# The small products of a delta-net at other places in the program

## The chip, the core and the metric

The kernel runs on one core of a Trainium2 chip. Its time is the device time of one execution in microseconds (us). TensorE (PE) does the matmuls and transposes, VectorE (DVE) the elementwise work and the rounding remainders, ScalarE (ACT) functions and copies, GpSimd (POOL) a few elementwise steps; SyncE (SP) issues the DMAs.

## What is computed

Four decoder layers on x of 256 tokens by 1024 channels, float32. Each adds half a SwiGLU FFN (1024 to 2816 and back), a mixer, and half of a second FFN; a last RMS norm ends it. Layer i has mixer i mod 3: the gated delta-net in layers 0 and 3, stick-breaking attention in 1, sparse attention in 2. The change touches the delta-net alone:

```python
def gated_deltanet(h, w_in, conv_w, a_log, dt_bias, norm_g, w_out):
    proj = h @ w_in                                  # q, k, v, gate z, and 8+8 columns for beta and decay
    qkv = silu(causal_depthwise_conv(proj[..., :3 * GDN_DIM], conv_w))     # 4 taps
    q, k, v = 8 heads of 128 each;  q = l2norm(q) * 128 ** -0.5;  k = l2norm(k)
    beta = sigmoid(b_logit);  g = -exp(a_log) * softplus(a + dt_bias)
    o = chunk_gated_delta_rule(q, k, v, g, beta)     # triangular solves, then a recurrence
    o = rmsnorm(o, norm_g) * silu(z)
    return o @ w_out
```

h is the normalised x. The kernel multiplies the gain in first and the row factor 1/rms after the projections.

## The kernel before

**Matmuls in three parts.** Float32 products are made of three matmuls of a reduced type: a weight is split into a hi half (`h`, ACT, line 175) and a lo half (`l`, DVE, line 176), x likewise, and `mm3` adds hi*hi, lo*hi and hi*lo. All matmuls are issued in line 43 and all transposes in line 56, so a row is told by its tiles, not by its line. A weight chunk of 1 MB (128 x 2048) is loaded by one DMA, split in four pieces of 512 columns, and gives a tile of 256 output channels by 256 tokens: 2 halves x 8 k tiles x 3 = 48 matmuls of 256 columns into a bank of tag G. There are three raw buffers, ten for hi and ten for lo halves, and four PSUM banks each of tags G and A.

**The delta-net.** `gdn_order` lists 16 projection chunks as (kind, c), kind 0 for keys, 1 values, 2 queries, 3 gates; a chunk c holds two heads. After each chunk comes its follow-up: `conv2` (a multiply with the norm factor, four taps on ACT, POOL and DVE, Silu) for keys, values and queries, a multiply and Silu for gates. Then generators do the small products with banks of tag A. `rstd` sums the squares of x and makes the norm factor `rb` by a rsqrt of nine small DVE steps and a transpose ("spread", line 242). `gates` makes beta, the decays and the matrices E, and needs `rb`. `keys(c)` transposes the keys (`bk`, line 488), sums their squares on ACT (492), takes a rsqrt on DVE (line 494; steps of lines 213 to 217), waits for the gates, and after a lag `g_new` scales `bk` (501), spreads the rsqrt (502), scales the keys (503), and multiplies them with themselves (509); from there a triangular inverse goes by doubling. `queries(c)` transposes and multiplies with the keys; `delta(c)` waits for all inverses and is a chain of small products, the last of which waits for the gate of c. `out_proj` multiplies the heads with the output weights, with banks of tag G.

**Order.** The program is written out by a planner. `mm` adds 256/2400 to `now` for a matmul of 256 columns. A generator yields a lag after which its next step is due (or a condition); `add` gives the first lag. `pump`, called after every second k tile of a projection, runs the steps that are due, from the first six generators. `wait` runs steps until a condition holds, with `now` set ahead. A compiler pass then orders each engine's instructions by this order of the program and by its own estimate of when operands are there; each engine works through its own queue in that order.

```python
    g_key, g_val, g_qry, g_del, g_new, g_inv, g_out, g_mul = 9.0, 6.0, 6.0, 8.0, 2.8, 1.0, 7.5, 1.0
            yield self.g_new
            self.wait(lambda: "rb" in st)
                self.add(keys(c), self.g_key)
```

These are the lag of the keys' second step (276, 500), the wait for the norm behind the first chunk (655), and the first lag of the keys (666).

Of the kernel before, what the change touches and what calls it, by code (L numbers as in the profile page):

```python
# [20 lines left out]
P = 128  # L21
T = 256
D = 1024
KT = D // P
# [41 lines left out]
class Trunk:  # L66
# [177 lines left out]
    def rstd(self, st, lat=4.6, power=False):  # L244
# [18 lines left out]
        else:  # L263
# [9 lines left out]
    lag, width, burst = 1.0, 6, 5  # L273
    lat_sum, lat_power = 5.2, 2.4
    dsa_width = 4
    g_key, g_val, g_qry, g_del, g_new, g_inv, g_out, g_mul = 9.0, 6.0, 6.0, 8.0, 2.8, 1.0, 7.5, 1.0
    s_qk, s_sp, s_att = 2.5, 5.5, 1.3

    gdn_order = ((0, 0), (0, 1), (0, 2), (3, 0), (0, 3), (3, 1), (2, 0), (1, 0), (1, 1), (1, 2), (1, 3),
                 (2, 1), (3, 2), (2, 2), (2, 3), (3, 3))  # L280
    korder = (0, 2, 4, 6, 1, 3, 5, 7)

    def tiles2(self, pieces, xg, order=None):

        b = self.bank("G")
        for m in range(2):
            for q, j in enumerate(order or self.korder):
                b.mm3(b.t[:, m * T:(m + 1) * T], self.sub(pieces, m * D + j * P, P), xg[j], q == KT - 1)
                if q % 2:
                    self.pump()  # L290
        return b
# [89 lines left out]
    def gdn(self, i, n):  # L381
        nc, a = self.nc, self.a
# [10 lines left out]
        bah, bal = self.small("bah", [P, 8, 16], F32R, 1), self.small("bal", [P, 8, 16], F32R, 1)  # L393
        self.split(bah, bal, wba)
        xg = self.norm_in(n)
        st = {}
        self.add(self.rstd(st))


        bba = self.bank()  # L400
        for j in range(KT):
            bba.mm3(bba.t[:16, :T], (bah[:, j], bal[:, j]), xg[j], j == KT - 1)


        four = lambda name: self.big.tile([P, 4, 4, P], F32, name=name, tag="b8")
        LL = self.big.tile([P, 4, 2, 4, P], F16, name="LL", tag="b8")
        XX = self.big.tile([P, 4, 2, 4, P], F16, name="XX", tag="b8")
# [8 lines left out]
        dl, ea = self.small("dl", [P, 4, 2], bufs=1), self.small("ea", [P, 4, 2], bufs=1)  # L416

        def gates():
            ba = self.pad
            nc.vector.tensor_mul(ba[:16], bba.t[:16, :T], st["rb"][:16])  # L420
            bt = self.bank()
            for t in range(2):
                bt.tr(bt.t[:, t * P:(t + 1) * P], ba[:, t * P:(t + 1) * P])
            v = bt.v4()[:, :2, :16].rearrange("p t (s c m) -> p s c t m", s=2, c=4)
            self.act_set("natural_log_exp_and_others")
            for t in range(2):
                nc.scalar.activation(beta[:, :, t], v[:, 0, :, t], AF.Exp, scale=-1.0)
                nc.vector.tensor_add(z[:, :, t], v[:, 1, :, t], ad[:, 1].rearrange("p (c m) -> p c m", m=2))
            nc.vector.tensor_scalar(beta, beta, 1.0, None, op0=ALU.add)
            nc.vector.reciprocal(beta, beta)  # L430
            nc.scalar.activation(e, z, AF.Abs)
            nc.scalar.activation(e, e, AF.Exp, scale=-1.0)
            nc.scalar.activation(e, e, AF.Ln, bias=self.ones[:, :1])
            nc.vector.scalar_tensor_tensor(sp, z, 0.0, e, op0=ALU.max, op1=ALU.add)
            self.tc.keep_in_program_order(nc.scalar.activation(ea, ad[:, 0].rearrange("p (c m) -> p c m", m=2), AF.Exp))
            for t in range(2):
                nc.vector.scalar_tensor_tensor(g[:, :, t], sp[:, :, t], -1.0, ea, op0=ALU.mult, op1=ALU.mult)
            yield 3.0
            bg = self.bank()
            bg.mm(bg.t[:, :16], triu, g.rearrange("p c t m -> p (c t m)"))  # L440
            bg.mm(bg.t[:, 16:24].rearrange("p (c m) -> p c m", m=2), self.ones, g[:, :, 0])
            G = bg.t[:, :16].rearrange("p (c t m) -> p c t m", c=4, t=2)
            nc.vector.tensor_scalar(nG, G, -1.0, None, op0=ALU.mult)
            nc.vector.tensor_add(dl, bg.t[:, 16:24].rearrange("p (c m) -> p c m", m=2), nG[:, :, 0])
            nc.scalar.activation(dl, dl, AF.Exp)
            nc.scalar.activation(eG, G, AF.Exp)
            nc.vector.tensor_copy(e, G)

            for c in range(4):
                yield 0.8  # L450
                b = self.spread([e[:, c, t, m:m + 1] for t in range(2) for m in range(2)])
                nc.scalar.activation(eGb[:, c], b.v4()[:, 2:], AF.Exp)
                nc.vector.tensor_add(E[:, c], b.v4(), nG[:, c].rearrange("p t m -> p (t m)")[:, :, None].to_broadcast([P, 4, P]))
                nc.gpsimd.affine_select(out=E[:, c], in_=E[:, c], compare_op=ALU.is_ge, fill=-BIG, base=0, pattern=[[0, 4], [1, P]],
                                        channel_multiplier=-1)
                nc.scalar.activation(E[:, c], E[:, c], AF.Exp)
            self.act_set("silu_and_others")
            st["gates"] = True
# [3 lines left out]
        def conv2(b, kind, c, dst):  # L462

            pc = self.pcs[cnt[0] % 2]
            cnt[0] += 1
            nc.vector.tensor_mul(pc[:, :, 3:], b.v2(), st["rb"][:, None, :].to_broadcast([P, 2, T]))  # L466

            base = (1, 2, 0)[kind] * 8 + 2 * c
            w = lambda m, o: conv[:, base + m, o:o + 1]
            tap = self.w5("tap").rearrange("p (m t) -> p m t", m=2)  # L470
            for m in range(2):
                nc.scalar.activation(dst[:, m], pc[:, m, 0:T], AF.Copy, scale=w(m, 0))
                nc.scalar.activation(tap[:, m], pc[:, m, 1:1 + T], AF.Copy, scale=w(m, 1))
            nc.gpsimd.tensor_add(dst, dst, tap)
            for m in range(2):
                for o in (2, 3):
                    nc.vector.scalar_tensor_tensor(dst[:, m], pc[:, m, o:o + T], w(m, o), dst[:, m], op0=ALU.mult, op1=ALU.add)  # L477
            nc.scalar.activation(dst, dst, AF.Silu)
# [7 lines left out]
        def keys(c):  # L486
# [10 lines left out]
            nc.gpsimd.tensor_mul(A, E[:, c], beta[:, c].rearrange("p t m -> p (t m)")[:, :, None].to_broadcast([P, 4, P]))  # L497
            ks = self.small("ks", [P, 2], tag="ms")
            nc.vector.tensor_mul(ks, y[:, :2], dl[:, c])
            yield self.g_new  # L500
            nc.vector.tensor_mul(kx[:, 0, c], bk.v4()[:, :2], ks[:, :, None].to_broadcast([P, 2, P]))
            b = self.spread([y[:, t * 2 + m:t * 2 + m + 1] for m in range(2) for t in range(2)])
            nc.vector.tensor_mul(k2, k2, b.v2())
# [16 lines left out]
            b = self.bank()  # L520
# [27 lines left out]
            b = self.bank()  # L548
# [6 lines left out]
            for src, dst in ((XT, X1), (X1, XF[:, c])):  # L555
                yield self.g_inv
                b = self.bank()
# [6 lines left out]
        def values(c, vT):  # L564
            b = transposed(vT)
            nc.scalar.activation(v[:, c], b.v4(), AF.Copy)
            st["v", c] = True
            yield 0
# [82 lines left out]

        heads, gz = {}, {}
        for kind, c in self.gdn_order:
            b = self.tiles2(self.chunk(a["gdn_in"][i, kind * 4 + c], pool=self.pool_lo), xg)
            self.wait(lambda: "rb" in st)
            if kind == 0:
                if c == 0:
                    self.add(gates())
                    late = b
                    continue  # L660
                if c == 1:
                    self.wait(lambda: "gates" in st)
                    conv2(late, 0, 0, kT[:, 0:2])
                    self.add(keys(0), self.g_key)
                conv2(b, 0, c, kT[:, 2 * c:2 * c + 2])
                self.add(keys(c), self.g_key)
            elif kind == 1:
                vT = self.w5("vT").rearrange("p (m t) -> p m t", m=2)
                conv2(b, 1, c, vT)
                self.add(values(c, vT), self.g_val)  # L670
            elif kind == 2:
                conv2(b, 2, c, qT[:, 2 * c:2 * c + 2])
                if c == 0:
                    oh, ol = self.b8("oh", F32R), self.b8("ol", F32R)
                self.add(queries(c), self.g_qry)
                self.add(delta(c), self.g_del)
            else:
                gz[c] = self.small("z", [P, 2, T], bufs=4)
                nc.vector.tensor_mul(gz[c], b.v2(), st["rb"][:, None, :].to_broadcast([P, 2, T]))
                nc.scalar.activation(gz[c], gz[c], AF.Silu)  # L680
# [537 lines left out]
```

## Time and profile before

| | |
|---|---|
| runs | 2054.35, 2075.12, 2082.24 us; median 2075.12 |
| profiled execution | 2066.59 us, of which 2064.6 us are the span of its instructions |
| PE, DVE, ACT, POOL busy in the span | 97%, 78%, 63%, 8% |
| granted TensorE clock | 0.996 of full speed, mean of the span |

Times in rows are microseconds from the start of the span, durations in ns where marked. A wait is idle time of an engine right before an instruction, put down to what released it. PE's ends are modelled and matmuls overlap, so their spacing is read from starts.

### The profile page before, as it was taken

What the parts mean: (1) busy time and instruction counts of PE and PEld (TensorE: products, weight loads), DVE (VectorE), ACT (ScalarE), POOL (GpSimd) and SP (SyncE); (2) the same over time, 40 slices, a digit from 0 to 9 for tenths busy, and PEclk for the clock granted to TensorE, in tenths of its full rate; (3) what the DMA queues carried; (4) which work ended last, traced back from release to release, by engine and by line L of the source; (5) the groups of instructions that cost most, each with busy time, mean ns of one, the idle gap of its engine ahead of it and who ended that gap; (6) DMA issues with size and microseconds to landing.
All of it is one profiled execution on the core that took longest, in us unless ns stands there. A gap on an engine that the chain in (4) does not pass through costs nothing.

```text
span 2064.6 us, 43653 instructions
## 1 busy us (share of the span) xinstructions
PE 2009.8 (97%) x17578; PEld 1978.6 (96%) x17578; DVE 1603.2 (78%) x3413; ACT 1305.8 (63%) x2804; POOL 163.8 (8%) x150
## 2 busy tenths in 40 slices
PE   8999899999999999999999998999999998999998
PEld 8999889999999989999999997999999998999998
DVE  8778898877877776866787779877787789988665
ACT  6656776666666666655666665666666667766554
POOL 1001411100100010100010023100010014201000
PEclk9999999999999999999999999999999999999999
DMA  7554323555555543555555542455555543235552
GB/s 273 191 199 170 107 104 124 184 195 193 180 209 186 202 168 139 196 184 184 184 190 199 187 161 88 165 187 201 189 195 190 198 170 103 103 123 184 184 184 82
DMA packets 52619, 353.93 MB, mean 171 GB/s; under 512 B 6976, under 2 KB 7872, under 8 KB 10688
## 3 DMA queue, kind: packets, MB, share of 16 engines
q1 hardware_dynamic: 52128, 350.49, 47.9%
q8 instruction: 137, 2.24, 0.4%
q10 hardware_dynamic: 288, 0.66, 0.1%
q14 instruction: 66, 0.54, 0.1%
HBM read 350.07 MB, written 1.05 MB: 170 GB/s over the span
## 4 chain that ended last, share of the span: by engine, by line
PE 83%; DVE 11%; ACT 3%; issue 2%; POOL 1%; DMA 0%; SPq 0%; ACTq 0%; DVEq 0%; POOLq 0%
PE bankG L43 56%; PE bankA L43 26%; DVE l L176 4%; ACT x L227 1%; DVE kT L477 1%; PE bankA L56 1%; ACT h L175 1%; DVE x L228 1%; DVE qT L477 0%; DVE x L313 0%; DVE rs_y L217 0%; DVE vT L477 0%; DVE pc L466 0%; DVE rs_t L215 0%; ACT sq L249 0%
## 5 line engine op out<-in xcount | busy, mean ns | idle before, releaser
L43 PE MATMUL bankG<-x,h 128*128 128x256 f32 x7008 | 1257.3, 280 | 9.1 <-ACT x L227 6.1
L176 DVE TENSOR_TENSOR l<-r,h 128x512 fp32r<-128x512 f32 x1328 | 936.2, 713 | 398.9 <-ACT h L175 396.8
L175 ACT ACTIVATE h<-r 128x512 fp32r<-128x512 f32 x1328 | 822.1, 626 | 575.7 <-PE bankG L43 329.1
L43 PEld LDWEIGHTS bankG<-x,h 128*128 128x128 f32 x7008 | 1077.6, 189 | 11.5 <-ACT x L227 6.4
L43 PE MATMUL bankG<-x,l 128*128 128x256 f32 x3504 | 978.4, 279 | 0.1
L43 PEld LDWEIGHTS bankG<-x,l 128*128 128x128 f32 x3504 | 659.9, 188 | 0.4 <-DVE l L176 0.3
L43 PE MATMUL bankA<-ah,h 128*128 128x256 f32 x1408 | 390.9, 278 | 0.0
L43 PE MATMUL bankA<-al,h 128*128 128x256 f32 x1408 | 390.9, 278 | 0.0
L43 PE MATMUL bankA<-ah,l 128*128 128x256 f32 x1408 | 390.8, 278 | 0.0
L43 PEld LDWEIGHTS bankA<-al,h 128*128 128x128 f32 x1408 | 266.0, 189 | 0.1
L43 PEld LDWEIGHTS bankA<-ah,h 128*128 128x128 f32 x1408 | 264.4, 188 | 0.1
L43 PEld LDWEIGHTS bankA<-ah,l 128*128 128x128 f32 x1408 | 264.4, 188 | 0.0
L341 DVE TENSOR_TENSOR e<-e,bankG 128x256 f32<-128x256 f32 x352 | 145.5, 414 | 0.9 <-ACT e L340 0.9
L340 ACT ACTIVATE e<-bankG 128x256 f32<-128x256 f32 x352 | 133.3, 379 | 7.9 <-PE bankG L43 6.3
L250 POOL TENSOR_TENSOR sq<-sq 128x512 f32<-128x512 f32 x12 | 15.5, 1290 | 1445.0 <-ACT sq L249 1445.0
L353 DVE TENSOR_TENSOR e<-e,rb 128x512 f32<-128x512 f32 x176 | 119.8, 685 | 0.0
L204 ACT ACTIVATE ah<-e 128x256 fp32r<-128x256 f32 x176 | 73.2, 417 | 22.1 <-DVE e L355 22.0
L354 ACT ACTIVATE e<-e 128x256 f32<-128x256 f32 x176 | 70.9, 404 | 14.3 <-DVE e L353 14.3
L355 DVE TENSOR_TENSOR e<-e 128x256 f32<-128x256 f32 x176 | 73.6, 419 | 0.5 <-ACT e L354 0.5
L205 DVE TENSOR_TENSOR al<-e,ah 128x256 fp32r<-128x256 f32 x176 | 73.6, 419 | 0.5 <-ACT ah L204 0.5
L43 PE MATMUL bankG<-oh,h 128*128 128x256 f32 x256 | 73.1, 286 | 0.1
L43 PE MATMUL bankG<-oh,l 128*128 128x256 f32 x256 | 71.3, 279 | 0.0
(292 smaller groups left out, 1683.0 us busy)
## 6 DMA issues: line engine op xcount, KB each, us to landing
r<-in_ffn SPq DMA_DIRECT2D x262, 1024.0 KB, 4.8
r<-in_gdn_in SPq DMA_DIRECT2D x32, 1024.0 KB, 4.8
r<-in_gdn_out SPq DMA_DIRECT2D x8, 1024.0 KB, 4.8
r<-in_sb_qk SPq DMA_DIRECT2D x8, 1024.0 KB, 4.8
r<-in_sb_v SPq DMA_DIRECT2D x4, 1024.0 KB, 5.0
r<-in_sb_out SPq DMA_DIRECT2D x4, 1024.0 KB, 4.8
r<-in_dsa_out SPq DMA_DIRECT2D x4, 1024.0 KB, 5.3
r<-in_dsa_in SPq DMA_DIRECT2D x3, 1024.0 KB, 4.8
```

The lines of the kernel that those rows point to most:

```text
L43: self.nc.tensor.matmul(out, lhsT, rhs, start=self.fresh, stop=stop, skip_group_check=True)
L56: self.nc.tensor.transpose(out, x, self.k.ident)
L175: self.nc.scalar.activation(h[:, :pw], src, AF.Copy)
L176: (self.nc.gpsimd if pool else self.nc.vector).tensor_sub(l[:, :pw], src, h[:, :pw].bitcast(F32))
L204: self.nc.scalar.activation(dh, src, AF.Copy)
L205: self.nc.vector.tensor_sub(dl, src, dh.bitcast(F32))
L227: self.nc.scalar.activation(xh, self.x[:, j], AF.Copy, scale=g)
L340: nc.scalar.activation(e[:, m * T:(m + 1) * T], b.t[:, :T], AF.Copy)
L341: nc.vector.tensor_add(e[:, m * T:(m + 1) * T], e[:, m * T:(m + 1) * T], b.t[:, T:])
L353: nc.vector.tensor_mul(e2, e2, st["rb"][:, None, :].to_broadcast([P, 2, T]))
L354: nc.scalar.activation(e[:, :T], e[:, :T], AF.Silu)
L355: nc.vector.tensor_mul(e[:, T:], e[:, T:], e[:, :T])
```

## The change

Six edits, all in the delta-net. The 24 small matmuls for beta and decay come behind the first projection chunk instead of ahead of it. That first chunk runs its k tiles in the outer loop, both halves of the output for each. The wait for the norm factor comes behind the second chunk instead of the first; `gates` is added behind the first and holds itself until `rb` is there. `g_new` is 4.8 instead of 2.8, and 3.0 more for chunk 0. The first lag of the keys of chunk 1 is 4.0 longer. In `gdn_order` the query chunks (2,2) and (2,3) come ahead of gate chunk (3,2).

```diff
-    g_key, g_val, g_qry, g_del, g_new, g_inv, g_out, g_mul = 9.0, 6.0, 6.0, 8.0, 2.8, 1.0, 7.5, 1.0
+    g_key, g_val, g_qry, g_del, g_new, g_inv, g_out, g_mul = 9.0, 6.0, 6.0, 8.0, 4.8, 1.0, 7.5, 1.0
...
-                 (2, 1), (3, 2), (2, 2), (2, 3), (3, 3))
+                 (2, 1), (2, 2), (2, 3), (3, 2), (3, 3))
...
-    def tiles2(self, pieces, xg, order=None):
+    def tiles2(self, pieces, xg, order=None, first=False):
...
+        if first:
+            for q, j in enumerate(self.korder):
+                w = [self.sub(pieces, m * D + j * P, P) for m in range(2)]
+                for i, o in ((0, 0), (1, 0), (0, 1)):
+                    for m in range(2):
+                        b.mm(b.t[:, m * T:(m + 1) * T], w[m][i], xg[j][o], q == KT - 1 and o == 1)
+                self.pump()
+            return b
...
-        bba = self.bank()
-        for j in range(KT):
-            bba.mm3(bba.t[:16, :T], (bah[:, j], bal[:, j]), xg[j], j == KT - 1)
...
         def gates():
+            yield lambda: "rb" in st
             ba = self.pad
...
-            yield self.g_new
+            yield self.g_new + (3.0 if c == 0 else 0.0)
...
-            b = self.tiles2(self.chunk(a["gdn_in"][i, kind * 4 + c], pool=self.pool_lo), xg)
+            b = self.tiles2(self.chunk(a["gdn_in"][i, kind * 4 + c], pool=self.pool_lo), xg, first=(kind, c) == (0, 0))
+            if kind == 0 and c == 0:
+
+                bba = self.bank()
+                for j in range(KT):
+                    bba.mm3(bba.t[:16, :T], (bah[:, j], bal[:, j]), xg[j], j == KT - 1)
+                self.add(gates())
+                late = b
+                continue
             self.wait(lambda: "rb" in st)
             if kind == 0:
-                if c == 0:
-                    self.add(gates())
-                    late = b
-                    continue
...
-                self.add(keys(c), self.g_key)
+                self.add(keys(c), self.g_key + (4.0 if c == 1 else 0.0))
```

## Rows read from the trace of the kernel before

**Rows 1.** The page: engines busy in the span, and the chain that ended last.

```profile
PE 2009.8 (97%) x17578; PEld 1978.6 (96%) x17578; DVE 1603.2 (78%) x3413; ACT 1305.8 (63%) x2804; POOL 163.8 (8%) x150
...
PE 83%; DVE 11%; ACT 3%; issue 2%; POOL 1%; DMA 0%; SPq 0%; ACTq 0%; DVEq 0%; POOLq 0%
```

**Rows 2.** Waits of PE, 184 to 362 (total, times, longest); then layer 3, 1672 to 1854.

```profile
PE bankA L56 <- DVE rs_y L217: 3.5, 4, 1.8
PE bankA L56 <- ACT kT L478: 3.1, 1, 3.1
PE bankA L56 <- DVE rs_t L216: 2.7, 1, 2.7
PE bankA L56 <- ACT qT L478: 2.2, 1, 2.2
...
PE bankA L56 <- DVE rs_y L217: 3.6, 4, 1.9
```

**Rows 3.** Delta-net in stretches: PE, PEld, DVE, ACT, POOL busy (count); clock, DMA.

```profile
184.00:200.00 16.00, 15.83 (x137) 14.96 (x137) 15.06 (x27) 12.56 (x23) 5.33 (x4) 1.00 0.32 111
200.00:224.00 24.00, 20.12 (x170) 19.36 (x169) 19.09 (x45) 16.19 (x39) 8.96 (x9) 1.00 0.40 147
224.00:236.00 12.00, 9.29 (x81) 9.13 (x80) 11.22 (x36) 10.70 (x34) 3.07 (x3) 0.97 0.26 89
236.00:248.00 12.00, 10.92 (x85) 10.48 (x84) 11.47 (x32) 6.96 (x18) 4.42 (x5) 0.88 0.25 89
248.00:270.00 22.00, 20.20 (x232) 19.27 (x231) 20.80 (x53) 15.16 (x37) 7.32 (x5) 1.00 0.35 124
270.00:300.00 30.00, 29.49 (x403) 27.77 (x404) 27.46 (x74) 20.57 (x53) 4.33 (x4) 1.00 0.16 55
```

**Rows 4.** Line 176 alone in a stretch: DVE busy (count), clock, DMA.

```profile
180.00:190.40 10.40, 3.91 (x6) 1.00 0.59 202
```

**Rows 5.** Tile l in stretches: PE, PEld, DVE busy (count), clock, DMA.

```profile
190.40:219.70 29.30, 17.67 (x63) 11.66 (x62) 11.80 (x14) 1.00 0.40 144
219.70:229.90 10.20, 4.72 (x18) 3.33 (x18) 1.94 (x2) 1.00 0.01 2
229.90:241.00 11.10, 2.94 (x11) 1.98 (x11) 4.89 (x8) 0.85 0.54 190
241.00:270.00 29.00, 15.82 (x55) 10.29 (x55) 8.00 (x12) 1.00 0.27 94
270.00:294.40 24.40, 7.33 (x23) 4.44 (x24) 1.36 (x2) 1.00 0.05 21
294.40:326.00 31.60, 15.22 (x55) 10.34 (x55) 14.80 (x21) 1.00 0.49 174
```

**Rows 6.** Chain in order of time: one chunk back to back in layer 0 (start, us).

```profile
49.13 5.44 PE bankA L43 x48
```

**Rows 7.** Timeline of PE: two spreads (start, us; idle before and its releaser).

```profile
203.01 0.43 PE L56 MATMUL bankA<-ident,rs_y 128*128 128x128 f32 x2 [0.60 <-DVE rs_y L217]
...
235.59 1.09 PE L56 MATMUL bankA<-ident,rs_y 128*128 128x128 f32 x4 [2.71 <-DVE rs_t L216]
```

**Rows 8.** Timeline of ACT: Silu of key chunk 1.

```profile
222.79 0.63 ACT L478 ACTIVATE kT<-kT 128x512 f32<-128x512 f32 x1 [2.29 <-DVE kT L477]
```

**Rows 9.** Timeline of DVE, 224 to 238.

```profile
224.78 1.38 DVE L176 TENSOR_TENSOR l<-r,h 128x512 fp32r<-128x512 f32 x1 [2.08 <-ACT h L175]
226.08 2.44 DVE L477 SCALAR_TENSOR_TENSOR kT<-pc,conv,kT 128x256 f32<-128x256 f32 x4
...
229.34 0.68 DVE L176 TENSOR_TENSOR l<-r,h 128x512 fp32r<-128x512 f32 x1
...
235.36 0.15 DVE L216 SCALAR_TENSOR_TENSOR rs_t<-rs_t,s 128x4 f32<-128x4 f32 x1
...
237.27 0.67 DVE L503 TENSOR_TENSOR kT<-kT,bankA 128x512 f32<-128x512 f32 x1
```

**Rows 10.** Timeline of ACT: Silu of query chunk 2.

```profile
338.35 0.63 ACT L478 ACTIVATE qT<-qT 128x512 f32<-128x512 f32 x1 [1.70 <-DVE qT L477]
```

## The prediction, made before the changed kernel ran

> **What bounds the kernel now.** I read the page first, then the waits of TensorE (PE), then stretches of the one stage that the edits touch. The page has PE at 97% of the span and a chain of work that is 83% PE and 11% VectorE (DVE) [rows 1]: the kernel is bound by matmuls, and only time in which PE stands can be won. The edits lie in the delta-net alone, which runs in layers 0 and 3. In layer 0 its PE work begins at about 190.4 us. The waits of PE there [rows 2] come to 11.5 us in four rows: 3.5 for the rsqrt of a norm (rs_y, the sum of four waits), 3.1 for key rows of chunk 1 (kT), 2.7 once more for an rsqrt (rs_t), 2.2 for query rows (qT). Rows of 0.6 us and less bring it to 12.7. Layer 3 repeats the list to within 0.1 us; one of its rows stands there. All four are transposes (L56) that stand in PE's queue before their operand is there, with projection matmuls behind them that need nothing new.
>
> To these waits belongs some clock. After two of them the granted clock of two 12 us stretches is 0.97 and 0.88 of full speed [rows 3], that is, part of them at the lower level of 1.2 GHz: 12 x 0.03 + 12 x 0.12 = 1.8 us. So one delta-net can give at most 12.7 + 1.8 = 14.5 us, both 29 us, 1.4% of the span.
>
> The second thing to read is what DVE does meanwhile. From 224 to 300 it is busy 70.95 of 76 us and PE 69.9 [rows 3]: in this stretch the two are about equally loaded. Each projection chunk needs four lo halves (l, L176) from DVE, and a piece of them feeds 12 matmuls, four of which read l. Counting l made against l consumed gives PE's stock. Six pieces were made in the last 10.4 us before the stage [rows 4], 14 by 219.7, two by 229.9, 8, 12 and 2 in the next stretches; matmuls on l number 63, 18, 11, 55 and 23 [rows 5]. So the stock is 20 - 63/4 = 4.2 pieces at 219.7, 22 - 81/4 = 1.8 at 229.9, and 44 - 170/4 = 1.5 at 294.4 (to half a piece: an instruction across a border counts on both sides, and a few records may be missing). Back to back, 48 matmuls take 5.44 us [rows 6], so one takes 0.1134 and a piece 12 x 0.1134 = 1.36 us. **At 294.4 PE can therefore be no more than 1.5 x 1.36 = 2.0 us earlier than it is, unless DVE is earlier too.** That cap decides my sum.
>
> **The change part by part.** Matmuls, transposes, DMAs and vector work are the same in number and shape. What moves is the place of the generators' steps in the program, and with it in each engine's queue. The sequence number (the planner's `now`) says only the order, not a time.
>
> *Start of the stage.* The 24 small matmuls of beta and decay go behind chunk (0,0), which now goes through the k tiles with both halves: 48 + 24 matmuls either way, cost nothing. PE is busy 15.83 of 16.00 us there [rows 3]; that is the most it can save (0.2 us). The normalised tiles come from DVE one by one. The loop by k tiles asks for the last one after 42 of 48 matmuls instead of after 21, which stands in for the cover that the 24 small ones gave. Without that cover PE would stand a few tenths.
>
> *Norm spread behind two chunks.* Today it waits 0.60 us at 203.01 [rows 7]. Now 48 + 24 + 48 matmuls come first: 190.4 + 120 x 0.1134 = 204.0, with the sums about 204.5. The wait of 0.6 goes, but everything that needs the norm starts 1.5 us later: gates, decay matrices, the convolutions of chunks 0 and 1. Queued behind these are the convolution taps on DVE, behind them the Silu of chunk 1 on ScalarE (ACT), which already stands 2.29 us for DVE at 222.79 [rows 8], and behind that Silu the next hi half (L175); DVE in turn stands 2.08 us for it at 224.78 [rows 9]. DVE is idle 4.9 us from 200 to 224 [rows 3] and can take up part. Cost between 0 and 1.5; I take 1.0, near the upper end, since the chain of dependent steps and not the amount of work carries it.
>
> *Keys of chunk 1 four units later.* The 3.1 us of kT go: PE finds the 4.2 pieces of stock instead, 5.7 us. Then lateness shows elsewhere. Piece 21 of the stage gets its lo half at 229.34 to 230.0, behind four convolution steps from 226.08 [rows 9]. PE begins it today at about 231 (20.25 pieces taken by 229.9, another 0.75 x 1.36 = 1.0 us) and, without the waits of 3.1 + 0.6, would at 227.3. So 2.7 us come back as a wait for L176, and the 1.0 from above is added. Net 0.0 of 3.7; bounds -1.5 (all given back, and the norm late by its whole 1.5) and 3.7.
>
> *Spread of the keys' norms: `g_new` 2.8 to 4.8, chunk 0 7.8.* In the program the spread of chunk 0 stood 2.8 units, or 26 matmuls at the planner's 0.107 each, behind its transposes; in the trace some 75 matmuls of the 81 PE instructions from 224 to 236 [rows 3] lie between, because the compiler's scheduler held it back by itself. With 7.8 it is put about where it already is. PE waits 2.71 us there because the rsqrt steps, tiny, alternate with lo halves of 0.68 us until 235.36 [rows 7, 9]. The keys of chunk 1 no longer alternate with them, and the eight squares of ACT that go with them come later: a little earlier done. Between 0 and 2.9; near the lower end, 0.9. The keys of chunks 2 and 3 wait some 0.9 and 1.8 today (the longest of the four is 1.8, and 3.5 - 0.6 - 1.8 leaves 1.1 for two) [rows 2]: 2.0 later covers either; bounds 0 and 2.7, I take 2.5.
>
> The parts ahead of 294 sum to 0.2 + 0.0 + 0.9 + 2.5 = 3.6, with at most the 1.8 of clock besides. The cap allows 2.0, plus what DVE gets faster. It stands 5.05 of 76 us from 224 to 300, 2.08 of them behind the Silu that gets later rather than earlier; I allow 0.3. **Ahead of 294: 2.3 us a delta-net**, clock included; bounds -1.5 and 12.1 (all its waits, 12.7 - 2.4, and the clock, 1.8).
>
> One rule of the Trainium skill makes this more. The page "TensorE: Matmul & The Clock Gate", section "Why this matters for your kernels", says that pauses of the engine between bursts of matmuls throw it back to the half rate, so a schedule without them keeps the clock. The two stretches at 0.97 and 0.88 behind the pauses agree [rows 3]. By that rule alone the whole 1.8 us would come on top, 2.3 to 4.1 a delta-net. The count of stock speaks against adding it: a faster PE only reaches the same lo half earlier.
>
> *Queries 2 and 3 ahead of gate 2.* Today the transposes of query chunk 2 stand 2.22 us for a Silu that ends its own wait at 338.35 [rows 2, 10], while DVE works through lo halves for the output projection; the chunk behind them, (3,3), has long been split. In the new order the two gate chunks follow both query chunks, so both sets of queries have 96 and more matmuls to be late behind. The Silu of the gate comes later, but the delta of chunk 2 asks for it only after its last transposes, by count behind (3,3). Here stock is no limit: from 294.4 to 326 DVE makes 21 lo halves and PE takes 55/4 = 13.8 [rows 5]. Between 0 and 2.4 (with the 0.2 for u); I take 2.2. What is late next is the tail of the output projection, whose deltas start a chunk earlier too.
>
> **Sum:** 2.3 + 2.2 = 4.5 a delta-net, 9.0 for both. Against the profiled execution, 2064.6 of span plus 2.0 around it = 2066.6, that gives 2057.6. Its time and the three runs are four times of one kernel, 2054.35 to 2082.24, mean 2069.6; the profiled one is 8.5 below the median of the three. I subtract from the mean of the four: **2060.6 us**.
>
> **The rivals.** (a) *All waits go.* If the scheduler, with the lags changed, also puts lo halves ahead of rsqrt steps and convolutions, the cap moves and PE runs through. For it: DVE's order is the scheduler's, made anew with every lag. Against: DVE has only 5 us of idle in 76, and what it does there doesn't shrink. It would give 24 to 29 for both, 26.5 in the middle: 2043. (b) *The lags do nothing*, since the scheduler already places the spreads by its own estimate (75 matmuls against 26), and the lo halves take the place of the 3.1 us. Then the late norm costs 1.0 a delta-net and qT gives some back: between -3 and +3, 2069. (c) *Slower, by banks.* The small products use four PSUM banks of one tag. The transposed keys hold one from their transposes to the multiply with ks. By the order of due times, chunks 0 and 1 now hold theirs when chunk 2 asks (by the planner's costs it is due at 36.3, the spread of chunk 0 at 39.7), so three of four are taken as the three spreads and then the three products of keys ask for one each. Each hand-over waits for a DVE multiply, 0.67 us for kT at 237.27 [rows 9], some six of them: 4.0 a delta-net, in place of the 2.3 ahead of 294. With queries' 2.2 kept that is +1.8 a delta-net, 3.6 in all: 2073.2; behind one more lo half each (0.68) it is +5.9 a delta-net, 12 in all, 2081.4. It decides when the hand-overs cost more than 2.2 a delta-net. Against it: no wait for a bank shows today, and the scheduler can fill with projections.
>
> The rule on which (c) leans has a page too: the Trainium skill, "Perfetto Trace Analysis", section "Optimization Strategy", says that a gap that repeats can mean that there is no SBUF or PSUM room for the next tile. No row of before shows such a gap; by that rule a gap before L56 ended by L501 or L503 would be one.
>
> **How the numbers follow.** Forecast 0.45; (a) 0.13; (b) 0.25; (c) 0.17. The forecast's own range is 2050 to 2067. The range for 8 in 10 takes in most of (a) and of (c), and the spread of the four times: 2042 to 2078. A measurement of this kernel can tell about 2%, 41 us, from no change. Both delta-nets together can give 29, and (c) takes 12, so faster by more has 0.02, slower by more 0.02, within 0.96.
>
> **What would show it.** Right: no wait of PE for kT or qT in rows like [rows 2]; a new one for l L176 near 226 to 230; rs waits smaller but there; the delta-net's stretch 4 to 5 us shorter; the clock near 236 at 0.9 or more. Wrong: waits of 10 us gone and l never late (a); L56 or key products waiting for L501 or L503 (c); the transposes of kT(1) still waiting for the Silu (b). I would be wrong above all if the scheduler reorders DVE's and ACT's queues, which I held fixed.

## The result and the profile after: slower by 0.7%

The changed kernel takes 2074.51 us in the median of 20 runs (2066.93 to 2087.99), the one before 2056.44 in 20 runs beside them (2052.64 to 2082.24). The ratio is **1.0070, 95% interval 1.0051 to 1.0090**. I had forecast 9 us less; it is some 14 us more (10 to 19 by the interval). Three runs below (one each of the kernel before, a_pre and c_key1) lie more than 1.5% above their kernel's fastest and are left out of ratios and means.

The profiled execution has a span of 2072.5 us, 7.9 more than before. Spans of single executions are a poor measure here (last section), so I compare the delta-net itself: from the last matmul of the FFN in front of it to the last of its output projection. The timeline of PE after, in layer 0 (start, us):

```profile
198.09 0.28 PE L43 MATMUL bankA<-al,h 128*128 128x256 f32 x1
...
388.62 0.28 PE L43 MATMUL bankG<-ol,h 128*128 128x256 f32 x1
```

That is 190.5 us, and 190.3 in layer 3 (1689.8 to 1880.2). The same two matmuls stand 183.6 and 183.8 us apart before (190.29 to 373.87 in layer 0). **Each delta-net is 6.7 us longer** in the mean of the two, 13.4 for both, which is of the size of the ratio: 13.4 / 2056 = 0.65%.

The waits of PE in the delta-net after, layer 0 (total, times, longest), where [rows 2] has those of before; layer 3 repeats them to 0.1 us:

```profile
PE bankA L56 <- ACT kT L482: 5.1, 3, 2.1
PE bankA L43 <- DVE u L626: 2.1, 2, 1.2
PE bankA L56 <- DVE rs_y L217: 2.1, 3, 0.9
PE bankG L43 <- DVE l L176: 1.5, 2, 1.0
PE bankA L43 <- DVE rr L619: 1.4, 1, 1.4
PE bankA L43 <- ACT XX L549: 1.2, 3, 0.4
PE bankA L43 <- DVE R L557: 1.0, 1, 1.0
```

The wait for qT is gone, that for rs_t too, rs_y is down from 3.5 to 2.1. In their place three sets of key transposes (kT) wait where one did, and the chains of small products wait for their own vector and scalar steps (XX and R of the inverse; u and rr of `delta`). All together PE stands 16.6 us, before 12.9: 3.7 more.

The rest, in this execution, is clock. The stretches after, from 34 to 110 us into the delta-net (columns as in [rows 3]):

```profile
232.10:244.10 12.00, 8.05 (x67) 7.69 (x68) 9.54 (x30) 9.42 (x34) 4.04 (x4) 1.00 0.13 37
244.10:256.10 12.00, 10.49 (x86) 9.83 (x85) 12.00 (x39) 7.25 (x17) 2.19 (x4) 1.00 0.30 104
256.10:278.10 22.00, 20.96 (x250) 19.57 (x249) 21.21 (x55) 15.93 (x40) 7.38 (x8) 1.00 0.32 117
278.10:308.10 30.00, 25.64 (x324) 23.84 (x323) 25.80 (x67) 17.98 (x46) 2.79 (x2) 0.83 0.21 72
```

Before, the stretches that answer to the first two had 0.97 and 0.88, and the last one 1.00 with PE busy 29.49 us [rows 3]. After, those two are at full clock and the last one has a mean of 0.83. At 1.2 GHz, half of full speed, that is some 10 of the 30 us at the lower level. It can have cost 30 x 0.17 = 5.1 us at most, against 1.7 before. PE also stands in that time: from 284.10 to 294.34 the granted clock is 0.50 and PE busy 8.25 of 10.24 us, before 0.51 from 235.40 to 238.81 and 3.04 of 3.41. Counting busy time alone the clock cost 4.1 against 1.5 us. So 3.7 of waits and 2.6 to 3.4 of clock stand beside the 6.9 of layer 0.

**The clock's share is that of one execution.** Its mean granted clock is 0.993, and 0.996 in the profiled execution of the kernel before: 14.5 against 8.3 us lost in the span (1 less the clock, times the span). The 20 runs after have a mean of 0.9939, 12.8 us. 116 runs of the kernel before, timed beside the experiments, lost 10.3 to 11.6 us on average in their four groups. So on average the clock is worth only 1.2 to 2.5 us of the 14, for both delta-nets together. With the waits of the profile, 2 x 3.7 = 7.4, that makes 9 to 10; what makes the rest isn't known, and that the two profiled delta-nets sum to 13.4 is in part chance.

**Why there.** Count the stock of lo halves as in the prediction. Tile l in the first 80 us of the delta-net and in the 11 us behind them, before and then after (PE, PEld, DVE busy with counts, clock):

```profile
190.30:270.30 80.00, 41.25 (x145) 27.26 (x144) 26.63 (x35) 0.98 0.32 115
270.30:281.40 11.10, 4.03 (x13) 2.57 (x14) 0.68 (x1) 1.00 0.08 31
```

```profile
198.10:278.10 80.00, 39.33 (x144) 26.46 (x144) 22.65 (x30) 1.00 0.30 106
278.10:289.20 11.10, 0.28 (x1) 0.14 (x1) 0.00 (x0) 0.77 0.01 1
```

With the six pieces made ahead [rows 4], 6 + 35 - 145/4 = 4.75 pieces lie ready before, 6 + 30 - 144/4 = 0 after. DVE is as busy (71.5 against 72.4 us of the 80) but has made five lo halves fewer and small products in their place. Then both enter a stretch in which DVE makes none or one. Before, PE lives on its stock, 13 matmuls on l. After it has **one in 11 us**, and does little but the small products of the inverses, standing again and again for the step before. PE after, timeline:

```profile
284.36 0.37 PE L43 MATMUL bankA<-Y,XX 128*128 128x64 f16 x4 [0.37 <-ACT XX L549]
285.34 0.40 PE L43 MATMUL bankA<-hf,XX 128*128 128x64 f16 x4 [0.61 <-DVE XX L544]
...
289.99 0.58 PE L43 MATMUL bankG<-x,l 128*128 128x256 f32 x1 [0.97 <-DVE l L176]
```

DVE after, timeline around the wait's end:

```profile
269.75 0.68 DVE L176 TENSOR_TENSOR l<-r,h 128x512 fp32r<-128x512 f32 x1
...
288.46 0.87 DVE L481 SCALAR_TENSOR_TENSOR vT<-pc,conv,vT 128x256 f32<-128x256 f32 x2
289.25 1.88 DVE L176 TENSOR_TENSOR l<-r,h 128x512 fp32r<-128x512 f32 x3
```

Between 269.75 and 289.25 there is no other L176. The kernel before has such a gap too, 17.6 us from 272.45 to 290.05. But there it begins 82.2 us into the delta-net, and 71.7 us in the kernel after, and PE still had 4.75 pieces at 80 us. The load and ACT weren't late: when the gap began, ACT had made six hi halves more (174 from the span's start, L175) than DVE lo halves (168), and DVE didn't stand before it began the one at 289.25. What held the lo halves back is the order of DVE's queue.

**Where the queries' gain went.** The Silu of qT no longer holds PE, but the convolution taps of the same queries now stand ahead of the delta chain in DVE's queue. DVE after, timeline:

```profile
338.83 1.67 DVE L481 SCALAR_TENSOR_TENSOR qT<-pc,conv,qT 128x256 f32<-128x256 f32 x4
340.42 0.41 DVE L619 TENSOR_TENSOR rr<-v,bankA 128x256 f32<-128x256 f32 x1
...
351.63 1.66 DVE L481 SCALAR_TENSOR_TENSOR qT<-pc,conv,qT 128x256 f32<-128x256 f32 x4
353.21 0.41 DVE L626 TENSOR_TENSOR u<-bankA,beta 128x256 f32<-128x256 f32 x1
```

PE waits 1.39 us for that rr and 1.18 for that u. Four more taps of qT stand ahead of another u at 328.01, which costs 0.93. So the 2.2 of qT came back as 3.5 (u and rr together).

**The late norm.** ACT after, timeline: the norm factor rb and the first Silu of the keys:

```profile
213.29 0.37 ACT L268 ACTIVATE rb<-bankA 128x256 f32<-128x256 f32 x1
...
229.55 0.63 ACT L482 ACTIVATE kT<-kT 128x512 f32<-128x512 f32 x1
```

The same two before:

```profile
203.48 0.38 ACT L268 ACTIVATE rb<-bankA 128x256 f32<-128x256 f32 x1 [0.81 <-PE bankA L56]
219.01 0.63 ACT L478 ACTIVATE kT<-kT 128x512 f32<-128x512 f32 x1
```

From the delta-net's start rb comes at 15.2 us, before at 13.2 (203.48 - 190.3); the Silu at 31.5, before at 28.7 (219.01). The 1.5 I had worked out is 2.0 at rb and 2.7 at the keys.

### The profile page after: what moved, and what is told of

It reads as the page before. It is cut to its first block, busy times and chain, and to the rows that moved or that the text cites. A ratio compares the mean times of both kernels' runs of the same rounds, so it can differ in the third digit from the quotient of the medians.

```text
span 2072.5 us, 43670 instructions
## 1 busy us (share of the span) xinstructions
PE 2009.5 (97%) x17578; PEld 1975.6 (95%) x17578; DVE 1599.8 (77%) x3413; ACT 1302.4 (63%) x2804; POOL 157.7 (8%) x150
## 4 chain that ended last, share of the span: by engine, by line
PE 81%; DVE 11%; ACT 4%; issue 2%; POOL 1%; DMA 0%; SPq 0%; ACTq 0%; DVEq 0%; POOLq 0%
PE bankG L43 55%; PE bankA L43 25%; DVE l L176 2%; DVE kT L481 1%; ACT h L175 1%; ACT x L227 1%; PE bankA L56 1%; DVE x L228 1%; DVE qT L481 1%; DVE x L321 1%; DVE rs_t L215 0%; DVE vT L481 0%; DVE pc L470 0%; DVE rs_y L217 0%; DVE rs_t L216 0%
## 5 line engine op out<-in xcount | busy, mean ns | idle before, releaser
L43 PE MATMUL bankG<-x,h 128*128 128x256 f32 x7008 | 1256.5, 280 | 10.2 <-ACT x L227 6.7
L176 DVE TENSOR_TENSOR l<-r,h 128x512 fp32r<-128x512 f32 x1328 | 933.0, 710 | 399.8 <-ACT h L175 398.0
L175 ACT ACTIVATE h<-r 128x512 fp32r<-128x512 f32 x1328 | 822.2, 626 | 587.0 <-PE bankG L43 348.0
L43 PEld LDWEIGHTS bankG<-x,h 128*128 128x128 f32 x7008 | 1077.9, 189 | 12.9 <-ACT x L227 7.0
```

The source lines that it names most:

```text
L43: self.nc.tensor.matmul(out, lhsT, rhs, start=self.fresh, stop=stop, skip_group_check=True)
L175: self.nc.scalar.activation(h[:, :pw], src, AF.Copy)
L176: (self.nc.gpsimd if pool else self.nc.vector).tensor_sub(l[:, :pw], src, h[:, :pw].bitcast(F32))
```

## Experiments

Each was timed against the kernel before on the same chip, in five rounds. For the profiled execution: the two delta-nets' lengths, PE's idle time and the time lost to the clock in the first one (12.9 and 1.7 before), both counted as above (the clock by its upper count), and the stock at 80 us. The last column is the clock once more, in all runs behind the ratio: 1 less the mean granted clock, times the span, for the whole program.

| run | ratio, 95% interval | delta-nets, us | idle | clock | stock | clock lost, all runs |
|---|---|---|---|---|---|---|
| before | 1 | 183.6, 183.8 | 12.9 | 1.7 | 4.75 | 10.3 to 11.6 |
| after | 1.0070 (1.0051 to 1.0090) | 190.5, 190.3 | 16.6 | 5.1 | 0 | 12.8 |
| p_order | 1.0015 (0.9992 to 1.0039) | 183.9, 183.2 | 13.2 | 1.7 | 4.75 | 10.1 |
| p_gnew | 1.0020 (0.9998 to 1.0042) | 185.6, 185.9 | 12.9 | 3.5 | 2.75 | 9.1 |
| p_key1 | 1.0021 (0.9991 to 1.0052) | 185.1, 184.3 | 13.2 | 5.2 | 5.0 | 12.1 |
| p_norm | 1.0057 (1.0033 to 1.0081) | 186.2, 187.0 | 12.2 | 5.2 | 3.5 | 14.3 |
| u_norm | 1.0036 (1.0011 to 1.0060) | 187.7, 186.6 | 14.3 | 1.7 | 2.25 | 8.8 |
| u_lags | 1.0046 (1.0020 to 1.0072) | 185.2, 187.3 | 12.8 | 3.5 | 3.25 | 11.7 |
| n_first | 1.0005 (0.9982 to 1.0028) | 185.1, 183.9 | 13.5 | 3.4 | 4.5 | 12.6 |
| n_wait | 1.0030 (1.0007 to 1.0053) | 185.0, 187.5 | 13.0 | 1.7 | 3.5 | 14.0 |
| a_pool | 1.0098 (1.0063 to 1.0134) | 192.2, 192.1 | 18.4 | 3.4 | | 11.3 |
| b_pool | 1.0160 (1.0131 to 1.0188) | 198.6, 196.6 | 22.8 | 7.0 | | 20.6 |
| a_pre | 1.0018 (0.9989 to 1.0047) | 186.4, 186.9 | 13.6 | 1.7 | 1.5 | 7.0 |
| b_pre | 1.0018 (0.9992 to 1.0044) | 183.5, 183.9 | 13.4 | 1.7 | 4.75 | 11.2 |
| c_norm | 1.0064 (1.0029 to 1.0099) | 188.6, 188.0 | 15.8 | 1.7 | 3.75 | 8.8 |
| c_key1 | 1.0026 (1.0004 to 1.0048) | 187.7, 187.6 | 13.0 | 5.2 | 0.25 | 10.2 |

Clock figures are sums over seven stretches and good to about a microsecond. Length less idle less clock is 168.8 to 169.0 before and after, 166.7 to 171.7 over all runs, so the two columns carry most of what differs, not all. And the clock of one execution is in part chance: n_wait, whose two delta-nets have the same order and 13.0 and 13.3 us of idle, loses 1.7 us in layer 0 and 5.1 in layer 3.

**One edit alone, in the kernel before.** The lines are those of the change, shortened:

```diff
p_order  +  (2, 1), (2, 2), (2, 3), (3, 2), (3, 3))
p_gnew   +  g_new = 4.8;   yield self.g_new + (3.0 if c == 0 else 0.0)
p_key1   +  self.add(keys(c), self.g_key + (4.0 if c == 1 else 0.0))
p_norm   +  small matmuls behind chunk (0,0), k tiles outermost, gates added there,
            wait for rb behind the second chunk
```

> The kernel before with the new gdn_order alone (queries 2 and 3 ahead of gate 2). Theory 1, the lags bunch the key chains and projections run out of lo halves: this edit is innocent, 0 to -4 us for both delta-nets (the wait of 2.2 for qT goes), ratio 0.998 to 1.000. Theory 2, the late norm does it: the same. Theory 3, the order does it: the delta chains now stand with only gate chunks around them, new waits for u and rr of some 3 us a delta-net, +6 us, ratio 1.003.

> The kernel before with g_new 4.8 and 3.0 more for chunk 0, alone. Theory 1: the spreads of chunks 0, 1 and 2 come together, three inverse chains run in step, the stretch behind 270 loses waits and clock: +5 to +10 us for both, ratio 1.002 to 1.005. Theory 2: nothing, 1.000. Theory 3: nothing, 1.000.

> The kernel before with the first lag of the keys of chunk 1 at 13 instead of 9, alone. Theory 1: the wait of 3.1 for kT goes or is split, chunk 1 comes next to chunk 2; between -4 and +4 us for both, ratio 0.998 to 1.002. Theory 2: the wait goes, -2 to -4 us, 0.998 to 0.999. Theory 3: as theory 2.

> The kernel before with the start edits alone: small matmuls behind the first chunk, first chunk by k tiles, norm spread behind two chunks, gates held until the norm is there. Theory 1: gates and convolutions some 2 us later, partly hidden: +1 to +4 us for both, ratio 1.000 to 1.002. Theory 2: the late norm carries the loss: +8 to +14 us, ratio 1.004 to 1.007. Theory 3: 1.000 to 1.001.

Three edits alone can't be told from no change, and none is shown to be faster. The start edits alone are slower by 0.57%, the most of the four, and their interval overlaps that of the whole change; their profiled delta-nets are 2.6 and 3.2 us longer, about half of what that ratio says. What the waits say is more. In p_order, PE's waits in the delta-net:

```profile
PE bankA L56 <- DVE rs_y L217: 3.8, 4, 1.8
...
PE bankA L56 <- ACT qT L478: 1.5, 2, 0.8
...
PE bankA L43 <- ACT junk L629: 0.5, 1, 0.5
```

Of qT's 2.2 us 0.7 go, and 0.5 return as a wait for a sum of squares (junk). In p_gnew the two rsqrt rows fall from 6.2 to 3.2, as forecast, and waits that [rows 2] doesn't have take their place:

```profile
PE bankA L56 <- DVE rs_y L217: 3.2, 4, 1.1
...
PE bankA L43 <- DVE Y L535: 1.1, 2, 0.7
PE bankA L43 <- DVE kT L503: 0.8, 2, 0.5
PE bankA L43 <- DVE XX L540: 0.8, 1, 0.8
```

In p_key1 the wait for kT goes and one for l comes, as forecast, 2.6 against the 2.7 worked out; the rsqrt rows stay at about their 6.2:

```profile
PE bankA L56 <- DVE rs_y L217: 6.5, 3, 4.2
PE bankG L43 <- DVE l L176: 2.6, 1, 2.6
```

but now the waits come close together: in this execution PE is busy 6.17 of 12 us in one stretch, and the two stretches at the place of the 0.97 and 0.88 of [rows 3] read

```profile
226.10:238.10 12.00, 6.17 (x52) 5.77 (x51) 11.45 (x25) 10.13 (x26) 4.00 (x3) 0.95 0.31 98
238.10:250.10 12.00, 11.08 (x77) 11.11 (x78) 10.69 (x34) 6.61 (x23) 2.15 (x3) 0.77 0.46 167
```

So every single edit moves its waits and leaves their sum at 12.2 to 13.2 us. The clock gets worse in three of these four executions, but over all runs only p_norm loses clearly more of it than the kernel before (14.3 us against 11.6).

**One group left out of the change.** u_norm keeps order and lags and has the start of before; u_lags keeps order and start and has the lags of before. In words:

```diff
u_norm   -  small matmuls behind chunk (0,0), k tiles outermost, wait behind the second chunk
u_lags   -  g_new 4.8, 3.0 for chunk 0, 4.0 for chunk 1
```

> The changed kernel with the four start edits undone (so both lags and the order alone). A delta-net's PE work takes 183.6 us before, 190.5 after; alone, the lags cost 2.0 and 0.9 to 1.5, the start edits 2.6 to 3.2, the order 0. If the edits only add: 186.5 to 187. If start and lags need each other (the keys' chains run dry only when all come late): 184 to 186 here and the most of the loss gone, ratio to before 1.001. If the lags alone make the dry stretch: 189 to 190, waits for the inverse's tiles and clock 0.83 behind 270 as after.

> The changed kernel with both lags undone (start edits and order alone). If the edits only add: 186.5 us a delta-net, ratio 1.003. If start and lags need each other: the same, with the stretch from 80 to 110 us of the delta-net at full clock. If the start edits carry the loss by themselves: 189 to 190.

u_norm gives back 6.5 and u_lags 8.3 of the 13.4 us of the two delta-nets; by the ratios it is half and a third, and both intervals overlap that of the whole change. u_norm is slower than the kernel before without any start edit, u_lags and p_norm without any new lag, so no group carries the loss by itself. The rows for u and rr appear at this size in u_norm (2.2 and 1.4) and in no kernel with the old lags: u_lags and p_order have 1.5 for qT in their place. It is the new lags together with the earlier queries that put the taps ahead of the delta chain.

**The start taken apart.** n_first has the small matmuls behind the first chunk and the loop by k tiles, with the wait for rb where it was; n_wait has only the later wait.

```diff
n_first  +  self.wait(lambda: "rb" in st)      # ahead of self.add(gates()), behind chunk (0,0)
n_wait   +  if kind == 0 and c == 0: self.add(gates()); late = b; continue   # ahead of the wait
```

> Of the start edits only two: small matmuls behind the first chunk, first chunk by k tiles; the norm is waited for behind the first chunk as before. The start edits together cost 2.6 to 3.2 us a delta-net. If the late norm costs them: 183.5 to 184.5 here. If the moved small matmuls or the k tiles do: 186 to 187.

> Of the start edits only the other: the norm's wait behind the second chunk, gates held until it is there. If the late norm costs them: 185.5 to 187 here, convolutions some 2 us later and the clock below 0.8 in the stretch 34 to 46 us. Otherwise 183.5 to 184.5.

The new first chunk costs nothing that the ratio can tell (its profiled delta-nets are 1.5 and 0.1 longer); the later norm costs 0.30%, some 6 us, 1.4 in the delta-net of layer 0 and 3.7 in that of layer 3.

**Who makes the lo halves.** GpSimd makes one of the four lo halves of each projection chunk, in the kernel after (a_pool) and in the one before (b_pool).

```diff
-    pool_lo = ()
+    pool_lo = (1,)
```

> The changed kernel with the second of four lo halves of each projection chunk of the delta-net made by GpSimd in place of VectorE. It takes 16 x 0.6 = 9.6 us off VectorE in a delta-net; GpSimd is 8% busy and takes some 1.3 us for such a tile. Theory A, VectorE cannot make lo halves in time once the small products come bunched and late: waits for l and the dry stretch go, 190.5 falls by 3 to 7 us, clock back near 1.00. Theory B, only the chain norm to gates to keys is late: 190 to 191, nothing changes. Rival: GpSimd is late itself and PE now waits for its lo halves: 192 and more.

> The kernel before with the same lo half on GpSimd. Theory A: the waits of 2.7 and 1.8 for the rsqrt shrink, 183.6 falls by 2 to 4 us; less than in the changed kernel, since its stock never ran dry. Theory B: 183 to 184. Rival: 185 and more.

Both are slower than the kernel before, b_pool by 1.6%; a_pool's interval overlaps that of the changed kernel. Line 176 in b_pool, on GpSimd and on DVE (busy, mean ns):

```profile
L176 POOL TENSOR_TENSOR l<-r,h 128x512 fp32r<-128x512 f32 x14 | 20.8, 1488 | 38.2 <-ACT h L175 38.2
L176 DVE TENSOR_TENSOR l<-r,h 128x512 fp32r<-128x512 f32 x66 | 47.7, 734 | 7.7 <-ACT h L175 7.7
```

GpSimd takes twice as long for one, and its own steps of the convolutions come later behind it: the taps of qT and vT on DVE wait 2.0 and 2.3 us for GpSimd, before 0.8 and 0.7. The kernel before suffers more than the one after, so this doesn't test the stock; it shows that load taken off DVE by this way costs more than it gives.

**When the lo halves are made.** Nothing else changes here: a projection chunk is loaded and split in the program one chunk ahead of its matmuls, so its lo halves stand earlier in DVE's queue.

```diff
-        for kind, c in self.gdn_order:
-            b = self.tiles2(self.chunk(...), xg, ...)
+        load = lambda q: self.chunk(...)            # chunk q of gdn_order
+        ahead = load(0)
+        for q, (kind, c) in enumerate(self.gdn_order):
+            pieces, ahead = ahead, load(q + 1) if q < 15 else None
+            b = self.tiles2(pieces, xg, ...)
```

> The changed kernel with each projection chunk of the delta-net loaded and split one chunk earlier in the program (nothing else changes; VectorE's queue then has no longer 53 operations without a lo half where the inverses run, but 17, 21 and 13). Theory A, PE runs out of lo halves there: the stretch 80 to 110 us of the delta-net gets back 3 us of waits and 5 of clock, 190.5 falls to 183 to 186. Theory B, the late chain norm to gates to keys sets the length: 189 to 191, the waits turn up before or behind it.

> The kernel before with the same earlier split. Its queue hardly changes (longest run without a lo half 42 in place of 47). Both theories: 183 to 184.5.

The kernel before doesn't change (183.5 and 183.9 us); the one after gets 4.1 and 3.4 us back in a delta-net, and its ratio goes from 1.0070 to 1.0018. Tile l in a_pre, and then all engines in its stretch from 80 to 110 us:

```profile
191.70:271.70 80.00, 40.54 (x146) 27.54 (x146) 25.06 (x32) 0.98 0.30 106
271.70:282.80 11.10, 4.73 (x15) 2.84 (x15) 1.37 (x2) 1.00 0.28 95
```

```profile
271.70:301.70 30.00, 27.94 (x370) 25.88 (x366) 26.57 (x70) 19.98 (x50) 2.77 (x2) 1.00 0.21 72
```

15 matmuls on l instead of one in the 11 us, and the clock is at full speed where it was 0.83. (Idle and clock of the first delta-net fall by 6.4 us, its length by 4.1; the difference isn't accounted for.) Loads and hi halves move along with the lo halves, but the hi halves stood ready in the kernel after, and b_pre shows that the earlier split gains nothing by itself. So this test shows the cause of the larger half, the order in which DVE makes lo halves and small products: 7.5 of the 13.4 us come back, and the two ratios' intervals don't overlap. Over all runs a_pre loses 7.0 us of clock and the kernel after 12.8, so some half of what comes back (0.5%, 11 us) is clock. The stock at 80 us alone doesn't rank the kernels: a_pre has 1.5 pieces there, c_norm below 3.75 and is longer.

**What remains of it.** a_pre still waits 5.4 us for kT, 2.2 for u and 1.4 for rr. c_norm is a_pre with the wait for rb behind the first chunk again; c_key1 is a_pre without the 4.0 on chunk 1.

```diff
c_norm   +  self.wait(lambda: "rb" in st)      # behind chunk (0,0)
c_key1   -  self.g_key + (4.0 if c == 1 else 0.0)
c_key1   +  self.g_key
```

> The changed kernel with each weight chunk split one chunk ahead, and besides with the wait for the norm factor behind the first chunk as before. With the split alone the delta-net takes 186.4 and 186.9 us against 183.6 and 183.8 before, and PE waits 5.4 us for the transposed keys kT. Theory A: what remains comes from the late norm, because each step behind it starts late. Then the delta-net takes 184 to 185 us, the waits for kT fall below 4, and the ratio to before is 0.999 to 1.002. Theory B: what remains comes from the lags of the keys. Then it stays at 186 to 187 and the ratio at 1.001 to 1.004.

> The changed kernel with each weight chunk split one chunk ahead, and without the 4.0 on the first lag of the keys of chunk 1. Theory A (the late norm carries what remains): the delta-net stays at 186 to 187 us. Theory B (the lag of the keys of chunk 1 carries it, three sets of key transposes standing together): it falls to 184 to 185 us, and the waits for kT from 5.4 us to some 3.

Neither theory holds: in both kernels the profiled delta-nets are longer than a_pre's, not shorter (by 2.2 and 1.1 us, and by 1.3 and 0.7); by the ratios neither can be told from a_pre. In c_norm one wait for kT of 4.4 us and four for rs_y (4.1 together) take the place of three for kT; in c_key1 the stock is 0.25 at 80 us and the clock 0.72 and 0.94 in two stretches. Each edit, and each edit taken back, makes a new order of the queues, and in these runs the effects don't add. Which edit carries the last 2.8 us of a_pre's delta-net stays open (its ratio can't be told from 1); u and rr make 3.6 of them by their rows, less the 2.2 of qT that they replaced.

## Why the prediction was wrong

**The assumption that failed** is the one named last in it: that DVE's and ACT's queues keep their order. With it fell the term "ahead of 294", 2.3 gained: in the first 110 us of the delta-net PE is busy 97.2 us after and 99.9 before, so 2.7 us more of waits, and up to 3.4 of clock in the profiled execution. The term for the queries, 2.2 gained, became 1.0 us more of waits behind the 110 us.

The stock of lo halves was the right account, and I used it as a cap on gains only. It is as much a floor under losses: I put 1.5 pieces at 294.4, 104 us into the delta-net, and let the stock only grow, while the new order left none at 80 us, and PE had little to put between the inverse products. Nor is 294.4 the driest place of the old order: counted to 290.0, 36 pieces were made and 167 matmuls on l done, which leaves 6 + 36 - 167/4 = 0.25 pieces, 0.3 us and not 2.0.

**Start of the stage**, 0.2 gained: about right; n_first is at 1.0005.

**Norm spread behind two chunks**, cost 1.0 between 0 and 1.5: the mechanism was right and the term too small. It is 2.7 late at the first Silu of the keys, and alone costs 1.4 and 3.7 in the two delta-nets. The wait of 0.60 at the spread is gone, as forecast.

**Keys of chunk 1**, net 0.0 of 3.7: alone it did what was worked out (kT gone, 2.6 for l against 2.7 forecast). What else made p_key1 no faster isn't settled: its profiled execution loses 3.5 us more to the clock, its 12 runs 0.5. Together with the late norm the wait for kT didn't even go: three of 5.1.

**`g_new`**, 0.9 + 2.5: 3.0 of it was there alone, and 2.7 of it came back in waits for Y, XX and kT L503, which I had put under rival (c) only.

**Clock inside the cap**: I argued that clock could give no more than the cap, and didn't ask what it could take. In the profiled execution it took 2.6 to 3.4 us a delta-net, on average over the runs about 1: it should have been a term with a sign of its own, not a side remark. The Trainium skill, "TensorE: Matmul & The Clock Gate", section "Why this matters for your kernels", says that idle gaps of the engine between bursts of matmuls put it back to half rate. The trace agrees only in part: the longest pause of the delta-net after, 2.08 us at 234.01, leaves its stretch at 1.00, and the clock falls at 284.10 behind short waits (none above 0.44 us from 274 on, PE busy 2.40 of the last 3.60 us).

**Queries ahead of the gate**, 2.2 with stock no limit: qT went, but 3.5 came for u and rr. I checked the lo halves there and not the taps, which are in the same queue of DVE. Alone the edit is worth 0.2 of 2.2.

**The rivals.** (a), all waits go, is out. (b), the lags do nothing, is out by its time and because the lags did much, though its sign is there: the transposes of chunk 1's keys still wait 2.08 us for the Silu. (c) gave 2073 to 2081 and the time is inside (its change, 3.6 to 12 us, is less than the 14 measured), but not by its mechanism: waits for kT L503 (now L507) are 0.2 us after, so banks were not what ended them. That the range held the time is luck: it was wide for (c) and for the spread of four runs, and the sign was wrong.

**What would show it** named a wait for l near 226 to 230; after, it stands at 290.

## What to carry over

Where a second engine is as full as the first one (DVE 71 of 76 us against PE's 70 [rows 3]), a wait that is removed at one place comes back at the next one: 13 other orders of the same work (the two with GpSimd aside) left PE's idle time in the first delta-net between 12.2 and 16.6 us, against 12.9. Before moving a step, list everything that stands in the same vector queue, and work out the stock of what the matmuls need at the driest place, for the loss as well as for the gain. And price the clock as a term of its own, with a range and over many runs: 12 to 14 us of pauses went with between 1.7 and 5.2 us of it in single executions, even between the two delta-nets of one kernel (n_wait).

## What I had not expected of the hardware

**Two spacings at the same clock.** In the chain of before, in order of time, a chunk of 48 matmuls takes

```profile
868.67 5.65 PE bankA L43 x48
...
1055.68 5.44 PE bankA L43 x48
```

5.65 us in some stretches and 5.44 in others, 117.7 against 113.3 ns a matmul. The granted clock reads 1.00 in both, and PE is busy throughout:

```profile
868.00:1010.00 142.00, 142.00 (x1208) 142.00 (x1207) 98.91 (x187) 83.25 (x168) 0.00 (x0) 1.00 0.53 187
1055.00:1200.00 145.00, 145.00 (x1281) 145.00 (x1281) 104.94 (x198) 87.77 (x179) 0.00 (x0) 1.00 0.56 196
```

18 such chunks stand in the profile of before (868 to 1010 and from 1889 on), nine in that of after (51 to 204). They come at other places in each profiled execution. By the starts of its matmuls the first such stretch before lasts from 848 to 1035, and at 4.4 of 117.7 ns a matmul it costs about 7 us. The profile of before has one stretch more, which would account for the 5.5 us by which the spans differ less (7.9) than the delta-nets (13.4). What sets them is not known from these runs.

**GpSimd as a helper.** It was busy 8% of the span, which looked like room. A quarter of the lo halves of one stage given to it made the kernel before slower by 1.6%: 1488 ns each against 734.
